# Forgetting-attention values in three float32r passes, gathered by block of keys

## The chip, the cores and the metric

The kernel runs on one core of a Trainium2 chip. The metric is the device time of one execution in microseconds; a figure for a kernel is the median of its runs. TensorE (PE in the profile) multiplies matrices, its weight loads are listed apart as PEld; VectorE is DVE, ScalarE is ACT, GpSimd is POOL, and SP issues the loads of the weights.

## What is computed

The reference is a first transformer block and then two layers of a second one, on 512 positions of width 1024. The change is in the attention of the second block's two layers: 8 heads of 128, causal, with a gate per position and head whose logarithms are summed along the sequence (`c` below).

```python
c = jnp.cumsum(log_f, axis=1)
def one_block(args):                   # 128 queries, all 512 keys
    s = jnp.einsum('bhqd,bhkd->bhqk', q_i, k) * scale
    s = s + (c_i[..., :, None] - c[:, :, None, :])
    s = jnp.where(k_pos <= q_pos, s, -jnp.inf)
    p = jax.nn.softmax(s, axis=-1)
    return jnp.einsum('bhqk,bhkd->bhqd', p, v)
...
y_attn = forgetting_attention(q, k, v, log_f) @ w_o_attn[l]
```

In the same layer stand a gated linear recurrence (a convolution of width 4, two gates from block-diagonal products, a scan along the sequence), its output gate, two projections back, and two feed-forward blocks.

## The kernel before

All wide products (GEMMs) are done in three float32r passes: each operand is held as a high part `hi` (a cast to float32r) and a low part `lo` (the difference), and `mm3` issues hi·hi, hi·lo and lo·hi. These are the lines L229, L230 and L231, 512 columns wide. The weights are streamed from memory in chunks of 256 KB through a ring of four buffers: SP loads `raw`, ScalarE casts `hi` (L197), VectorE subtracts `lo` (L198).

`mix(l)` is the layer part that the change touches. It computes the recurrence's input, the gates (`rnn`: products L897 and L898 in plain fp32, two instructions each for 512 columns, their tanh and exp on ScalarE, scans L914 on VectorE), the row of summed gates `ct` (transposed by L1014, written to memory as `cdram`), and then, in two halves `hf` of four heads, the projections q, k and v of those heads. Their accumulators `a` (four banks of PSUM) are emptied by VectorE at L1027, into tiles `qk` for q and k and `v` for v; q and k are normalised and transposed (L393, L395). `attn` runs over the four heads. For each it broadcasts the gate row into `cb` by a DMA from GpSimd's queue (L874), makes score tiles `s` of 128 queries and 128, 256, 384 and 512 keys (`attn_scores`: product L830, gate L833, mask L835, softmax), and one tile behind it the values of each tile (`attn_values`): it transposes the 128x128 blocks of probabilities (L851) into a bank `xs`, copies them to `pT` (L853), and multiplies each block with the head's 128 columns of `v` in plain fp32 (L855), accumulating into a bank `xh`. These are 1+2+3+4 = 10 products of 128 columns per head, 16 heads in both layers. `xh` is copied to `x` (L869). Later, before the last projection `w_o_attn`, all eight outputs are split into hi and lo (L223, L224).

The program is not in the order of the text. A scheduler (Tile) orders each engine's instructions by data dependencies, buffers and priority (`hp` is high priority), so attention, gates and GEMMs are interleaved; each engine then works through its own queue in order, waiting on semaphores. Pools of a fixed number of buffers per name (`t=3, qk=5, v=6, cb=2, s=3, pT=2`) bound how far apart things can run.

Of the kernel before, what the change touches and what calls it, by code (L numbers as in the profile page):

```python
# [7 lines left out]
F32 = mybir.dt.float32  # L8
F32R = mybir.dt.float32r
U8 = mybir.dt.uint8  # L10
AF = mybir.ActivationFunctionType
OP = mybir.AluOpType
# [106 lines left out]
class Build:  # L119
# [721 lines left out]
        nc.vector.tensor_scalar(s, s, ri, None, op0=OP.mult)  # L841
        return st

    def attn_values(self, st, v, vc, i, o):

        nc = self.nc
        n = (i + 1) * 128
        pt = self.aux("xs")
        for j in range(i + 1):
            js = slice(j * 128, j * 128 + 128)  # L850
            nc.tensor.transpose(pt[:, js], st[:, js], self.ident)  # L851
        pT = self.t("pT")
        nc.scalar.copy(pT[:, :n], pt[:, :n])  # L853
        for j in range(i + 1):
            nc.tensor.matmul(o[:, i * 128:n], v[j][:, vc:vc + 128], pT[:, j * 128:j * 128 + 128],  # L855
                             start=(i == 0 and j == 0), stop=(i == 3 and j == 3), skip_group_check=True)

    def attn(self, qT, kT, v, hd0, ct, cdram):

        nc = self.nc  # L860
        out, todo = [], []

        def values(st, hd, i):
            if i == 0:
                out.append(self.aux("xh"))
            self.attn_values(st, v, (hd - hd0) * 128, i, out[-1])
            if i == 3:
                y = self.t("x")
                nc.scalar.copy(y, out[-1])  # L869
                out[-1] = y  # L870

        for hd in range(hd0, hd0 + 4):
            cb = self.t("cb")
            nc.gpsimd.dma_start(cb, cdram[hd:hd + 1, :].to_broadcast([128, 512]))  # L874
            for i in range(4):
                todo.append((self.attn_scores(qT[hd - hd0], kT[hd - hd0], i, hd, ct, cb), hd, i))
                if len(todo) > 1:
                    values(*todo.pop(0))
        values(*todo.pop(0))
        return out  # L880

    def rnn(self, xr, bd, l, hb, sp4):
# [66 lines left out]
    def mix(self, l):  # L949
        nc = self.nc  # L950
        h = self.hx
        with ExitStack() as ctx:
            lp = ctx.enter_context(self.tc.tile_pool(name=f"lp{l}", bufs=1))
            self.pool(ctx, f"mb{l}", hm=8, t=3, bq=1, qk=5, v=6, qkT=8, cb=2, s=3, pT=2)
            with self.hp():
                rt, rb = self.stats()
            hb = self.lined(lp, (128, 32), name="hb")
# [13 lines left out]
            ct = self.lined(lp, (128, 32), name="ct")  # L971
            cdram = self.dp.tile([8, 512], F32, name=f"cd{l}")
            with ExitStack() as c2:
# [12 lines left out]
                for m in range(0, 8, 2):  # L986
                    for a in self.pair("w_in_2", l, 8, MIX + m * 128, h):
                        y = scaled(a, "t")
# [9 lines left out]
            for k0 in (0, 4):  # L998
                hi, lo = self.w("w_in_2", l, k0, 4, 3072, 128)
# [14 lines left out]
                nc.tensor.transpose(ps[:, i * 8:i * 8 + 8], fc[:, i * 128:i * 128 + 128], self.ident[0:8, 0:8])  # L1014
            nc.vector.tensor_copy(ct, ps[:, 0:32])
            self.tap(f"fc{l}", fc)
            ya = []
            for hf in range(2):
                for n in range(3):
                    bq = self.t("bq")  # L1020
                    c = n * 1024 + hf * 512
                    nc.gpsimd.dma_start(bq, self.ap["brow"][l:l + 1, c:c + 512].to_broadcast([128, 512]))
                    ts = []
                    for tt, a in enumerate(self.tokens("w_in_2", l, c, h)):
                        v = self.t("v" if n == 2 else "qk")
                        with self.hp():
                            nc.vector.scalar_tensor_tensor(v, a, rt[:, tt:tt + 1], bq, op0=OP.mult, op1=OP.add)  # L1027
                        ts.append(v)
                    if n == 0:
                        qT = self.heads_T(ts, 4, 128, qg)  # L1030
                    elif n == 1:
                        kT = self.heads_T(ts, 4, 128, self.col(("k_norm_2", l)))
# [19 lines left out]
            for n, (o, wn) in enumerate(((3072, "w_o_rnn_2"), (2048, "w_o_attn_2"))):  # L1052
# [4 lines left out]
                for m in range(0, 8, 2):  # L1057
                    ga = self.pair("w_in_2", l, 8, MIX + o + m * 128, h)
                    yo = self.pair(wn, l, 8, m * 128, yh if n else yr)
                    for i in range(2):  # L1060
                        with self.hp():
                            s = scaled(ga[i], "t" if n else "hm")
# [109 lines left out]
```

## Time and profile before

| what | value |
|---|---|
| runs | 3414.32 to 3415.7 us, median 3415.19 us |
| profiled execution | 3415.62 us |
| span of its trace | 3413.8 us |
| PE busy | 3393.3 us (99%) |
| DVE busy | 1880.3 us (55%) |
| ACT busy | 1308.8 us (38%) |

The profiled execution is 1.8 us longer than the span that the trace covers, and 0.4 us over the median. A busy engine is one with an instruction in progress; matmuls are pipelined, so that consecutive ones overlap in the rows, and what one adds to the time is the distance from its start to the next start. The chain that ended last gives PE 97% of the span, DVE 2% and ACT 1%.

### The profile page before, as it was taken

What the parts mean: (1) busy time and instruction counts of PE and PEld (TensorE: products, weight loads), DVE (VectorE), ACT (ScalarE), POOL (GpSimd) and SP (SyncE); (2) the same over time, 40 slices, a digit from 0 to 9 for tenths busy, and PEclk for the clock granted to TensorE, in tenths of its full rate; (3) what the DMA queues carried; (4) which work ended last, traced back from release to release, by engine and by line L of the source; (5) the groups of instructions that cost most, each with busy time, mean ns of one, the idle gap of its engine ahead of it and who ended that gap; (6) DMA issues with size and microseconds to landing.
All of it is one profiled execution on the core that took longest, in us unless ns stands there. A gap on an engine that the chain in (4) does not pass through costs nothing.

```text
span 3413.8 us, 42019 instructions
## 1 busy us (share of the span) xinstructions
PE 3393.3 (99%) x15370; PEld 2769.7 (81%) x15370; DVE 1880.3 (55%) x3168; ACT 1308.8 (38%) x2284; POOL 164.6 (5%) x273
## 2 busy tenths in 40 slices
PE   9999999999999999999999999999999999999999
PEld 6887777888888888788888888888887788888887
DVE  7698654534444444876455444444447865454442
ACT  3335443423333333654333333333336544343331
POOL 0011100000000001121000000000010110000000
PEclk9999999999999999999999999999999999999999
DMA  6223533433333333232333333333333222433332
GB/s 217 72 75 105 155 112 111 130 96 97 98 95 94 97 118 106 89 91 90 112 96 96 97 98 96 96 97 99 102 124 94 87 90 81 122 95 99 96 104 91
DMA packets 179599, 351.30 MB, mean 103 GB/s; under 512 B 20672, under 2 KB 21952, under 8 KB 178368
## 3 DMA queue, kind: packets, MB, share of 16 engines
q1 hardware_dynamic: 172944, 328.53, 31.5%
q0 software_dynamic: 6160, 19.37, 1.9%
q8 instruction: 121, 1.98, 0.2%
q10 hardware_dynamic: 288, 0.72, 0.1%
q14 instruction: 86, 0.70, 0.1%
HBM read 342.21 MB, written 6.32 MB: 102 GB/s over the span
## 4 chain that ended last, share of the span: by engine, by line
PE 97%; DVE 2%; ACT 1%; issue 0%; DMA 0%; POOL 0%; SPq 0%; DVEq 0%; ACTq 0%
PE a L231 30%; PE a L229 30%; PE a L230 30%; PE xh L855 1%; PE xs L830 1%; PE xh L430 1%; PE xh L512 1%; PE xs L490 1%; PE xs L851 1%; PE xm L393 0%; DVE xc L895 0%; PE xh L506 0%; PE xh L469 0%; PE xs L897 0%; PE xs L898 0%
## 5 line engine op out<-in xcount | busy, mean ns | idle before, releaser
L198 DVE TENSOR_TENSOR lo<-raw,hi 128x512 fp32r<-128x512 f32 x1144 | 785.8, 688 | 1255.9 <-ACT hi L197 1240.4
L197 ACT CAST hi<-raw 128x512 fp32r<-128x512 f32 x1144 | 707.1, 619 | 1569.4 <-PE a L230 1271.2
L230 PE MATMUL a<-h,hi 128*128 128x512 f32 x2528 | 990.3, 392 | 0.0
L229 PE MATMUL a<-h,hi 128*128 128x512 f32 x2528 | 984.6, 392 | 2.3 <-ACT h L590 2.3
L231 PE MATMUL a<-h,lo 128*128 128x512 f32 x2528 | 983.3, 393 | 0.0
L229 PEld LDWEIGHTS a<-h,hi 128*128 128x128 f32 x2528 | 475.5, 188 | 106.1 <-issue 6.1
L231 PEld LDWEIGHTS a<-h,lo 128*128 128x128 f32 x2528 | 475.2, 188 | 105.4 <-issue 7.2
L230 PEld LDWEIGHTS a<-h,hi 128*128 128x128 f32 x2528 | 475.2, 188 | 101.5 <-issue 3.6
L229 PE MATMUL a<-act,hi 128*128 128x512 f32 x960 | 373.4, 389 | 0.0
L230 PE MATMUL a<-act,hi 128*128 128x512 f32 x960 | 373.4, 389 | 0.0
L231 PE MATMUL a<-act,lo 128*128 128x512 f32 x960 | 372.8, 389 | 0.0
L230 PE MATMUL a<-Y,hi 128*128 128x512 f32 x544 | 214.5, 394 | 0.0
L229 PE MATMUL a<-Y,hi 128*128 128x512 f32 x544 | 213.7, 393 | 0.0
L231 PE MATMUL a<-Y,lo 128*128 128x512 f32 x544 | 212.8, 391 | 0.0
L230 PEld LDWEIGHTS a<-act,hi 128*128 128x128 f32 x960 | 180.2, 188 | 37.4
L229 PEld LDWEIGHTS a<-act,hi 128*128 128x128 f32 x960 | 180.2, 188 | 37.4
L231 PEld LDWEIGHTS a<-act,lo 128*128 128x128 f32 x960 | 180.2, 188 | 37.4
L231 PE MATMUL a<-hi,h 128*128 128x512 f32 x512 | 204.6, 403 | 0.0
L230 PE MATMUL a<-lo,h 128*128 128x512 f32 x512 | 203.7, 398 | 0.0
L229 PE MATMUL a<-hi,h 128*128 128x512 f32 x512 | 199.2, 407 | 1.7 <-DVE qk L1027 1.7
L231 PEld LDWEIGHTS a<-Y,lo 128*128 128x128 f32 x544 | 102.2, 188 | 23.6 <-issue 2.1
L230 PEld LDWEIGHTS a<-Y,hi 128*128 128x128 f32 x544 | 102.1, 188 | 22.9 <-issue 2.0
(290 smaller groups left out, 3056.7 us busy)
## 6 DMA issues: line engine op xcount, KB each, us to landing
raw<-in_w_l SPq DMA_DIRECT2D x852, 256.0 KB, 2.6
raw<-in_w_first SPq DMA_DIRECT2D x284, 256.0 KB, 2.6
mr<-in_mod_b_ SPq DMA_DIRECT2D x32, 512.0 KB, 3.8
mq<-in_mod_a SPq DMA_DIRECT2D x8, 1024.0 KB, 7.5
xs<-x POOLq DMA_DIRECT2D x16, 256.0 KB, 2.3
cb<-cd POOLq DMA_DIRECT2D x16, 256.0 KB, 3.5
x<-xs POOLq DMA_DIRECT2D x16, 256.0 KB, 3.8
bq<-in_brow POOLq DMA_DIRECT2D x12, 256.0 KB, 3.8
```

The source lines that it names most:

```text
L197: nc.scalar.copy(hi, raw)
L198: nc.vector.tensor_tensor(lo, raw, hi.bitcast(F32), op=OP.subtract)
L229: mm(acc, w[0], x[0], start=start, stop=False)
L230: mm(acc, w[0], x[1], start=False, stop=False)
L231: mm(acc, w[1], x[0], start=False, stop=stop)
L430: mm(ps[:, i * 64:i * 64 + 64], k[:, s], q[:, s].rearrange("p (n c h) -> p n c h", c=2, h=h)[:, :, 1], start=True, stop=True)
L490: mm(z[:, o:o + n], q[pr, blk(i)], k[pr, :n], start=True, stop=True)
L512: mm(pt[pr, c], v[j][:, hd * 64:hd * 64 + 64], f[:, o + j * 128:o + j * 128 + 128], start=j == 0, stop=j == i, skip_group_check=True)
L830: nc.tensor.matmul(ps[:, :n], qT[:, ts], kT[:, :n], start=True, stop=True)
L851: nc.tensor.transpose(pt[:, js], st[:, js], self.ident)
L855: nc.tensor.matmul(o[:, i * 128:n], v[j][:, vc:vc + 128], pT[:, j * 128:j * 128 + 128], start=(i == 0 and j == 0), stop=(i == 3 and j == 3 ...
```

## The change

Values are no longer made per block of queries. All score tiles of a head are kept (`s` has five buffers), and `attn_values` runs once per head, over the four blocks j of 128 keys: it transposes that block of all score tiles which see it (4, 3, 2, 1 blocks), casts the result to `hi`, subtracts `lo`, and accumulates in three float32r passes over 512, 384, 256 and 128 columns. `v` is split into `hi` and `lo` after it is emptied into a tile `qk`, and lives in eight float32r tiles of a pool that is opened only after the gate row. The values of a head are issued in the middle of the next head's scores. The names `t`, `cb`, `v` and `s` get other numbers of buffers. Lines behind the change in the file have numbers lower by 4 (L1014 becomes L1010, L897 becomes L893, L913 and L914 become L909 and L910, L1027 becomes L1024, L198 stays).

```diff
@@ -841,42 +841,38 @@
         nc.vector.tensor_scalar(s, s, ri, None, op0=OP.mult)
         return st
 
-    def attn_values(self, st, v, vc, i, o):
-
-        nc = self.nc
-        n = (i + 1) * 128
-        pt = self.aux("xs")
-        for j in range(i + 1):
+    def attn_values(self, sts, v, vc):
+
+        nc = self.nc
+        o = self.aux("xh")
+        for j in range(4):
             js = slice(j * 128, j * 128 + 128)
-            nc.tensor.transpose(pt[:, js], st[:, js], self.ident)
-        pT = self.t("pT")
-        nc.scalar.copy(pT[:, :n], pt[:, :n])
-        for j in range(i + 1):
-            nc.tensor.matmul(o[:, i * 128:n], v[j][:, vc:vc + 128], pT[:, j * 128:j * 128 + 128],
-                             start=(i == 0 and j == 0), stop=(i == 3 and j == 3), skip_group_check=True)
+            n = 512 - j * 128
+            pt = self.aux("xs")
+            for i in range(j, 4):
+                nc.tensor.transpose(pt[:, (i - j) * 128:(i - j) * 128 + 128], sts[i][:, js], self.ident)
+            hi, lo = self.t("pT", F32R), self.t("pT", F32R)
+            nc.scalar.copy(hi[:, :n], pt[:, :n])
+            nc.vector.tensor_tensor(lo[:, :n], pt[:, :n], hi[:, :n].bitcast(F32), op=OP.subtract)
+            self.mm3(o[:, j * 128:], [a[:, vc:vc + 128] for a in v[j]], (hi[:, :n], lo[:, :n]), j == 0, j == 3)
+        y = self.t("x")
+        nc.scalar.copy(y, o)
+        return y
 
     def attn(self, qT, kT, v, hd0, ct, cdram):
 
         nc = self.nc
         out, todo = [], []
-
-        def values(st, hd, i):
-            if i == 0:
-                out.append(self.aux("xh"))
-            self.attn_values(st, v, (hd - hd0) * 128, i, out[-1])
-            if i == 3:
-                y = self.t("x")
-                nc.scalar.copy(y, out[-1])
-                out[-1] = y
-
         for hd in range(hd0, hd0 + 4):
             cb = self.t("cb")
             nc.gpsimd.dma_start(cb, cdram[hd:hd + 1, :].to_broadcast([128, 512]))
+            sts = []
             for i in range(4):
-                todo.append((self.attn_scores(qT[hd - hd0], kT[hd - hd0], i, hd, ct, cb), hd, i))
-                if len(todo) > 1:
-                    values(*todo.pop(0))
-        values(*todo.pop(0))
+                sts.append(self.attn_scores(qT[hd - hd0], kT[hd - hd0], i, hd, ct, cb))
+                if i == 1 and todo:
+                    out.append(self.attn_values(*todo.pop(0)))
+            todo.append((sts, v, (hd - hd0) * 128))
+        out.append(self.attn_values(*todo.pop(0)))
         return out
 
     def rnn(self, xr, bd, l, hb, sp4):
@@ -951,7 +947,7 @@
         h = self.hx
         with ExitStack() as ctx:
             lp = ctx.enter_context(self.tc.tile_pool(name=f"lp{l}", bufs=1))
-            self.pool(ctx, f"mb{l}", hm=8, t=3, bq=1, qk=5, v=6, qkT=8, cb=2, s=3, pT=2)
+            self.pool(ctx, f"mb{l}", hm=8, t=2, bq=1, qk=5, qkT=8, cb=1, s=5, pT=2)
             with self.hp():
                 rt, rb = self.stats()
             hb = self.lined(lp, (128, 32), name="hb")
@@ -1014,6 +1010,7 @@
                 nc.tensor.transpose(ps[:, i * 8:i * 8 + 8], fc[:, i * 128:i * 128 + 128], self.ident[0:8, 0:8])
             nc.vector.tensor_copy(ct, ps[:, 0:32])
             self.tap(f"fc{l}", fc)
+            self.pool(ctx, f"at{l}", v=8)
             ya = []
             for hf in range(2):
                 for n in range(3):
@@ -1022,10 +1019,10 @@
                     nc.gpsimd.dma_start(bq, self.ap["brow"][l:l + 1, c:c + 512].to_broadcast([128, 512]))
                     ts = []
                     for tt, a in enumerate(self.tokens("w_in_2", l, c, h)):
-                        v = self.t("v" if n == 2 else "qk")
+                        v = self.t("qk")
                         with self.hp():
                             nc.vector.scalar_tensor_tensor(v, a, rt[:, tt:tt + 1], bq, op0=OP.mult, op1=OP.add)
-                        ts.append(v)
+                            ts.append(self.split(v, "v") if n == 2 else v)
                     if n == 0:
                         qT = self.heads_T(ts, 4, 128, qg)
                     elif n == 1:
```

The scheduler moves instructions as a result. The first place is on TensorE, in the first layer, where the gate row is transposed (L1014 before, L1010 after; `xm` is the bank, `s2392` the row of gates). Around it stands the GEMM of q (accumulators `a2395` to `a2398`). Before:

```order
L229 MATMUL a2398_11235<-hi2406_11274,h2154_10144 128x512
L230 MATMUL a2398_11235<-lo2407_11275,h2154_10144 128x512
L1014 MATMUL xm2393_11224<-cst_74,s2392_11214 128x8 [waits DVE_49]
L1014 MATMUL xm2393_11224<-cst_74,s2392_11214 128x8 x3
L231 MATMUL a2398_11235<-hi2406_11274,h2155_10145 128x512
L230 MATMUL a2395_11232<-lo2410_11293,h2158_10155 128x512
L231 MATMUL a2395_11232<-hi2409_11292,h2159_10156 128x512
L229 MATMUL a2396_11233<-hi2409_11292,h2158_10155 128x512
```

After the change, with the waits on other engines in brackets:

```order
L230 MATMUL a2397_11237<-lo2410_11296,h2158_10155 128x512
L231 MATMUL a2397_11237<-hi2409_11295,h2159_10156 128x512
L1010 MATMUL xm2393_11224<-cst_74,s2392_11214 128x8 [waits DVE_49]
L1010 MATMUL xm2393_11224<-cst_74,s2392_11214 128x8 x3
L893 MATMUL xs2342_11035<-xc2341_11030,bd2251_10638 128x512 [waits DVE_49,Activation_49]
L894 MATMUL xs2343_11036<-xc2341_11030,bd2253_10646 128x512 [waits Activation_49]
L229 MATMUL a2398_11238<-hi2400_11241,h2111_9922 128x512 [waits DVE_49]
L230 MATMUL a2398_11238<-lo2401_11242,h2111_9922 128x512
```

The gates' products of the third convolution tile (L893 and L894, input `xc2341`) now stand directly behind the transposes; before, they stand 27 rows further down, behind GEMM passes.

The second place is on VectorE, where the four accumulators of v are emptied (`a2491` to `a2494`) and where the recurrence's last four scans stand (`hm2360` and others; L913/L909 multiplies, L914/L910 scans). Before:

```order
L1027 SCALAR_TENSOR_TENSOR v2519_11794<-a2491_11646,m2248_10617,bq2490_11644 128x512
L198 TENSOR_TENSOR lo2657_12218<-raw2655_12215,hi2656_12217 128x512
L1027 SCALAR_TENSOR_TENSOR v2520_11796<-a2492_11647,m2248_10617,bq2490_11644 128x512
L1027 SCALAR_TENSOR_TENSOR v2521_11798<-a2493_11648,m2248_10617,bq2490_11644 128x512
L1027 SCALAR_TENSOR_TENSOR v2522_11800<-a2494_11649,m2248_10617,bq2490_11644 128x512
L906 SCALAR_TENSOR_TENSOR abc2379_11151<-abc2379_11151,xc2376_11142 128x512
L905 SCALAR_TENSOR_TENSOR abc2380_11152<-xc2382_11158,abc2380_11152 128x512
L913 TENSOR_TENSOR abc2358_11091<-abc2358_11091,abc2359_11092 128x512
L913 TENSOR_TENSOR abc2365_11111<-abc2365_11111,abc2366_11112 128x512
L833 SCALAR_TENSOR_TENSOR s2525_11806<-xs2524_11804,ct_10633,cb2523_11802 128x128
L914 SCALAR_TENSOR_TENSOR hm2360_11093<-hm2360_11093,abc2358_11091 128x512
```

After:

```order
L909 TENSOR_TENSOR abc2358_11091<-abc2358_11091,abc2359_11092 128x512
L909 TENSOR_TENSOR abc2365_11111<-abc2365_11111,abc2366_11112 128x512
L909 TENSOR_TENSOR abc2372_11131<-abc2372_11131,abc2373_11132 128x512
L198 TENSOR_TENSOR lo2675_12241<-raw2673_12238,hi2674_12240 128x512
L910 SCALAR_TENSOR_TENSOR hm2360_11093<-hm2360_11093,abc2358_11091 128x512
L909 TENSOR_TENSOR abc2379_11151<-abc2379_11151,abc2380_11152 128x512
L910 SCALAR_TENSOR_TENSOR hm2367_11113<-hm2367_11113,abc2365_11111 128x512
L198 TENSOR_TENSOR lo2678_12259<-raw2676_12256,hi2677_12258 128x512
L910 SCALAR_TENSOR_TENSOR hm2374_11133<-hm2374_11133,abc2372_11131 128x512
L910 SCALAR_TENSOR_TENSOR hm2381_11153<-hm2381_11153,abc2379_11151 128x512
L1024 SCALAR_TENSOR_TENSOR qk2519_11797<-a2491_11649,m2248_10617,bq2490_11647 128x512
```

The four emptyings stood ahead of the scans; now the first of them stands behind all four multiplications, all four scans and two `lo` of weights, and goes into a tile `qk`.

The third place is on TensorE, at the last head of the layer (accumulator `xh2924` before, `xh2978` after) with the GEMM that the scheduler put next to it. Before, the last products:

```order
L230 MATMUL a3062_13915<-Y2664_12262,hi3065_13919 128x512
L855 MATMUL xh2924_13262<-pT2942_13317,v2816_12945 128x128 [waits Activation_49]
L855 MATMUL xh2924_13262<-pT2942_13317,v2817_12947 128x128
L855 MATMUL xh2924_13262<-pT2942_13317,v2818_12949 128x128
L855 MATMUL xh2924_13262<-pT2942_13317,v2819_12951 128x128
L231 MATMUL a3062_13915<-Y2663_12261,lo3066_13920 128x512 [waits DVE_49]
L229 MATMUL a3062_13915<-Y2667_12275,hi3065_13919 128x512
L230 MATMUL a3062_13915<-Y2668_12276,hi3065_13919 128x512
```

After the change, the end of the last head, and what follows (`Y3170`, `Y3171`, `Y3156` are hi and lo parts of attention outputs, `hi3198` weights of `w_o_attn`):

```order
L230 MATMUL xh2978_13395<-pT2987_13423,v2847_13018 128x256 [waits DVE_49]
L231 MATMUL xh2978_13395<-pT2986_13422,v2848_13019 128x256
L229 MATMUL xh2978_13395<-pT2989_13431,v2850_13024 128x128 [waits Activation_49]
L230 MATMUL xh2978_13395<-pT2990_13432,v2850_13024 128x128 [waits DVE_49]
L231 MATMUL xh2978_13395<-pT2989_13431,v2851_13025 128x128
L229 MATMUL a3186_14374<-Y3170_14296,hi3198_14432 128x512 [waits Activation_49]
L229 MATMUL a3187_14375<-Y3170_14296,hi3198_14432 128x512
L230 MATMUL a3186_14374<-Y3171_14297,hi3198_14432 128x512 [waits DVE_49]
L231 MATMUL a3186_14374<-Y3170_14296,lo3199_14433 128x512
L230 MATMUL a3187_14375<-Y3171_14297,hi3198_14432 128x512
L231 MATMUL a3187_14375<-Y3170_14296,lo3199_14433 128x512
L229 MATMUL a3216_14532<-Y3156_14268,hi3219_14536 128x512 [waits DVE_49]
```

Before, other GEMM passes of the output gates follow and the first use of `w_o_attn` is about 190 rows further down. Now the passes of `w_o_attn` follow immediately, and they wait for the casts of the attention's output.

## Rows read from the trace of the kernel before

**Rows 1.** First lines of the page: span, and the engines over all of it.

```profile
span 3413.8 us, 42019 instructions
...
PE 3393.3 (99%) x15370; PEld 2769.7 (81%) x15370; DVE 1880.3 (55%) x3168; ACT 1308.8 (38%) x2284; POOL 164.6 (5%) x273
```

**Rows 2.** Busy us by stretches: PE, PEld, DVE, ACT, POOL; then clock, DMA share, GB/s.

```profile
1000.00:1100.00 100.00, 100.00 (x443) 82.84 (x442) 47.45 (x73) 32.15 (x54) 0.00 (x0) 1.00 0.33 100
...
1400.00:1500.00 100.00, 98.76 (x458) 78.31 (x458) 84.01 (x154) 60.58 (x110) 12.52 (x16) 1.00 0.29 90
...
1450.00:1480.00 30.00, 30.00 (x146) 24.71 (x145) 29.52 (x61) 16.90 (x36) 4.98 (x6) 1.00 0.36 105
```

**Rows 3.** Who TensorE waited for: us in all, times, longest.

```profile
PE a L229 <- DVE qk L1027: 1.7, 2, 0.9
...
PE xm L393 <- ACT qkT L395: 0.8, 2, 0.4
```

**Rows 4.** TensorE in order of time, first head of attention: start us, us, instruction.

```profile
1456.79 0.27 PE L851 MATMUL xs<-cst,s 128*128 128x128 f32 x1
1456.90 0.81 PE L830 MATMUL xs<-qkT,qkT 128*128 128x384 f32 x2
...
1461.88 0.38 PE L855 MATMUL xh<-pT,v 128*128 128x128 f32 x2
1462.10 0.38 PE L851 MATMUL xs<-cst,s 128*128 128x128 f32 x2
```

**Rows 5.** Line L855, the products of the values.

```profile
L855 PE MATMUL xh<-pT,v x320: 270/275/275, 1461.9 to 2886.4; 128*128 128x128 f32 x160
```

**Rows 6.** TensorE in order of time, at the transposes of the gate row.

```profile
1368.38 0.41 PE L1014 MATMUL xm<-cst,s 8*128 8x8 f32 x4
1368.72 0.50 PE L231 MATMUL a<-hi,h 128*128 128x512 f32 x1
```

**Rows 7.** VectorE in order of time, same place.

```profile
1368.89 0.75 DVE L895 SCALAR_TENSOR_TENSOR xc<-xr,cv,xc 128x512 f32<-128x512 f32 x1
1369.55 1.29 DVE L198 TENSOR_TENSOR lo<-raw,hi 128x512 fp32r<-128x512 f32 x2
1370.75 0.75 DVE L895 SCALAR_TENSOR_TENSOR xc<-xr,cv,xc 128x512 f32<-128x512 f32 x1
```

**Rows 8.** TensorE in order of time, last gates of the first layer.

```profile
1437.98 1.02 PE L897 MATMUL xs<-xc,bd 128*128 128x512 f32 x2
1438.84 1.02 PE L898 MATMUL xs<-xc,bd 128*128 128x512 f32 x2
```

**Rows 9.** VectorE in order of time, around the same place.

```profile
1437.04 0.75 DVE L1027 SCALAR_TENSOR_TENSOR v<-a,m,bq 128x512 f32<-128x512 f32 x1 [2.08 <-PE a L231]
...
1444.35 1.29 DVE L913 TENSOR_TENSOR abc<-abc,abc 128x512 f32<-128x512 f32 x2 [1.11 <-ACT abc L911]
...
1445.83 1.22 DVE L914 TENSOR_TENSOR_SCAN hm<-hm,abc 128x512 f32<-128x512 f32 x1
1446.96 0.71 DVE L913 TENSOR_TENSOR abc<-abc,abc 128x512 f32<-128x512 f32 x1
1447.59 1.21 DVE L914 TENSOR_TENSOR_SCAN hm<-hm,abc 128x512 f32<-128x512 f32 x1
```

**Rows 10.** Groups by line and form: busy us, mean ns of one, idle before.

```profile
L224 DVE TENSOR_TENSOR Y<-x,Y 128x512 fp32r<-128x512 f32 x8 | 5.5, 688 | 2.7 <-PE a L230 2.6
...
L223 ACT CAST Y<-x 128x512 fp32r<-128x512 f32 x8 | 5.0, 620 | 2.9 <-PE a L230 2.9
...
L869 ACT COPY x<-xh 128x512 f32<-128x512 f32 x8 | 4.7, 581 | 7.0 <-PE xh L855 6.9
...
L853 ACT COPY pT<-xs 128x128 f32<-128x128 f32 x8 | 2.2, 269 | 1.5 <-PE xs L851 1.5
```

**Rows 11.** The broadcast of a gate row: its issue on POOL, and L874 to landing.

```profile
1468.58 0.57 POOL L874 DMA_DIRECT2D cb<-cd  x1 [0.19 <-issue]
...
DMA to landing us min/median/max: 3.3/3.5/4.4
```

## The prediction

> **What bounds the kernel now.** I read the head of the page first, then the windows, the waits of TensorE, and the timelines of the places that the change touches. The page shows TensorE busy for 3393.3 of 3413.8 us [rows 1]: it leaves 20 us in all, so the time is TensorE's work plus the few places where it stands still. The windows say the same by stretches: in a stretch of GEMMs alone, 443 float32r passes of 512 columns fill 100 us at a granted clock of 1.00, the upper level of 2.4 GHz, so one pass costs 0.226 us; in the stretch with gates and attention TensorE still has 98.76 of 100 us, while VectorE is at 84.01, and between 1450 and 1480 us VectorE has 29.52 of 30 [rows 2]. The wait list shows how little of the mix is lost: 1.7 us in two waits at the emptying of accumulators and 0.8 us in two at transposes, over both layers [rows 3]. So the prediction has two parts: what TensorE's work becomes, and which new waits arise in an order that had almost none.
>
> **The products removed.** In the first head, a product of values starts at 1461.88 and the next instruction at 1462.10: 0.22 us for one product of 128 columns, in two instructions [rows 4]. There are 160 of them, listed as 320 instructions [rows 5], so 35.2 us are removed. The transposes stay: 10 blocks per head either way.
>
> **The products added.** Each head now has 12 passes: three each of 512, 384, 256 and 128 columns. No float32r pass narrower than 512 columns is in the trace, so I bound it. By columns from 0.226 us [rows 2] the passes cost 0.226, 0.170 and 0.113 us, and the narrowest would cost 0.057, but every instruction of 128 columns in the trace, a transpose or half of an fp32 product, takes 0.11 us from start to start (1456.79 to 1456.90, and half of 0.22) [rows 4]. With 0.11 a head costs 3 x (0.226 + 0.170 + 0.113 + 0.110) = 1.86 us, all 16 heads 29.7, a gain of 5.5 us. If the narrowest pass costs what an fp32 product of its size does, 0.22, a head costs 2.19 us, all 35.0, a gain of 0.2 us. Between these ends neither is nearer, so I take the middle, a gain of 2.9 us.
>
> **The work beside it.** ScalarE's four copies per head become casts of four widths, the same total of columns. VectorE gains four subtractions per head (about 1.8 us, from 0.688 us for 512 columns by width [rows 10]) and four of v per half (2.8 us), so 10 us per half; ScalarE gains four casts of 0.620 us per half [rows 10]. Their cover is TensorE's GEMM work between. It is thin only where VectorE is already full [rows 2], which is the third rival. `cb` with one buffer means that a gate row is fetched only when the last score tile of the head before has been read: 0.57 us of issue and 3.5 us to landing [rows 11], 4.1 us in which GpSimd's queue holds the issue and VectorE's queue soon stands at the next gate addition, with `lo` parts of weights behind it. The cover is the weights already split; I count it at nothing, and with the third rival if the cover is gone.
>
> **The waits added.** Both layers have the same order, so each is counted twice.
>
> (a) The gates behind the transposed gate row. TensorE comes to L1014 at 1368.38 and goes on at 1368.72 [rows 6]. The next instruction will be the gates' product of `xc2341`, whose last convolution tap starts at 1370.75 now, with two `lo` (1.20 us) between it and the tap of 1368.89 [rows 7]. In the new order the two taps follow each other: the last starts at about 1369.55 and is ready at 1370.3. TensorE arrives at 1368.7, so it waits 1.6 us. Bounds: 1.0 if VectorE gets there a tap earlier, 2.4 if the `lo` of the following chunk, now behind the gates on VectorE, is late too.
>
> (b) The first emptying of v. Counted from 1439.70, where TensorE is through with the layer's last gates (L898 starts at 1438.84 and takes 0.86, as L897 did from 1437.98 [rows 8]), the first multiplication of the recurrence's end starts at 1444.35 [rows 9], 4.65 us later. In the new order VectorE then has four multiplications (0.61 each), four scans (1.13 each, 1445.83 to 1446.96), two `lo` (0.60 each, half of 1.20 [rows 7]) and the emptying, 0.75 [rows 9], before the accumulator is free: 4.65 + 2.4 + 4.5 + 1.2 + 0.75 = 13.5 us. Before, the emptying stood ahead of that and was begun at 1437.04. TensorE arrives at the first GEMM pass that needs this bank after 48 passes (10.85 us), eight transposes (0.88) and two score products (0.22 and 0.43, by columns from 0.86), 12.4 us. It waits 1.1 us; bounds 0 (VectorE 1.1 us quicker somewhere in that row) and 3 (the other three emptyings go through one spare `qk` tile each).
>
> (c) The end of the layer. The last head ended far from the first use of `w_o_attn`; now its passes stand directly ahead of it, and nothing is left to put between. The last block's cast to `hi` stands behind a weight's cast on ScalarE (about 0.5 us of wait), `lo` on VectorE follows (0.6), then the copy of the output, 0.581 us, and its cast, 0.620 [rows 10], with 0.3 of handing over: 1.5 us in which TensorE has nothing. Then 0.25 us for the output's `lo`, 0.688 less the two passes in front of it, and 0.5 until an accumulator is free: 3.3 us in all, of which the 0.5, 0.3 and 0.5 are estimates (about one ScalarE or VectorE instruction of these rows, or half of one, each). Bounds: 1.5 if only copy and cast remain, 4.5 if a weight's cast comes between each of them. A block's copy of 128 columns takes 0.269 us [rows 10], so the chain itself is not longer.
>
> (d) `t` with two buffers and the evictions of q and k, where waits of 0.9 and 0.4 us stand already [rows 3]: 0.6 us per layer, bounds 0 and 2.
>
> The sum is 1.6 + 1.1 + 3.3 + 0.6 = 6.6 us per layer, 13.2 in both, bounds 5 and 24. The profiled execution took 3415.6 us, 1.8 more than its span and 0.4 more than the median of the runs: 3415.6 - 2.9 + 13.2 = 3425.9, against the median 3425.5. With all bounds it would be 3414.7 to 3439.
>
> **A rule weighed.** The rows give 0.226 us for a pass of 512 columns in a running stream. The Trainium skill, TensorE: Matmul & The Clock Gate, section Back-to-back issue gap, gives for the isolated gap at full clock N/2.4 + 2.5 ns, by which 512, 384, 256 and 128 columns take an estimated 216, 162, 109 and 56 ns; a head would take 1.63 us and the gain would be 9.1 us. The trace has 226 where that has 216, and for 128 columns 110 where that has 56, so here the measurement decides; the sum stays at 2.9.
>
> **The rivals.** First: the waits are mostly covered and the narrow passes are cheap, because the semaphores named in the new order are met early by engines that run ahead. For it speaks that waits in the present order are 1.3 us per layer in all [rows 3]; against it, that the inputs of (a) and (c) are late by the trace's own times. The time is about 3415.2 - 5.5 + 5 = 3414.7, no change that shows: 0.2%, 6.8 us, is about what a measurement of this kernel can tell from none.
>
> Second, on the other side, faster: a narrow pass costs by its columns alone. Then a head costs 3 x (0.226 + 0.170 + 0.113 + 0.057) = 1.70 us, all 27.1, a gain of 8.1 us, 3407.1 without waits. It decides only if all new waits stay under 1.3 us (8.1 less 6.8), and (c) alone is more by its lower bound. Against it stands the 0.11 us of each 128-column instruction [rows 4].
>
> Third: VectorE becomes the bound in the first half of each layer. The 10 us more, with waits of up to 4.1 us for each gate row in front of `lo` parts, fall where it has 29.52 of 30 us [rows 2]. Uncovered, they put 20 us on the two layers, and with (a) and (c), 9.8, it is 3415.2 - 2.9 + 29.8 = 3442. Against it: over the whole first half TensorE's work between the same marks grows too, since GEMM passes are put there.
>
> Fourth: all float32r passes under 512 columns cost what fp32 does (0.86 us for 512 columns [rows 8]): 0.226 + 0.65 + 0.43 + 0.22, three times, 4.58 us per head, 73.3 in all, 38 more than before, with the waits 3466. Nothing in the rows speaks for it, but no row excludes it.
>
> **How the numbers follow.** The forecast has 0.56, the first rival 0.25, the second 0.08, the third 0.08, the fourth 0.03. The forecast's own range is 3417 to 3438. From 3411, which takes in the first rival, to 3439, the upper bound of the waits, about 0.8 is held; outside are most of the second, the third and the fourth. Faster is the second rival, 0.08; within 0.2% are the first and a twentieth from the forecast's lower end, 0.30; slower is the rest, 0.62.
>
> **What the changed profile would show.** The passes that read `pT`: starts 0.226, 0.17, 0.11 and 0.11 to 0.22 us apart, and 192 of them in all. A wait of TensorE at L893 of about 1.6 us in each layer, at L229 for the emptying L1024 of about 1, and at the last head's `pT`, at the first `Y` and its `lo`. VectorE under 100% between 1450 and 1500 us, or else waits of TensorE at `lo` of weights there. The prediction is wrong if those waits are under half their size, if the narrow passes lie outside 0.06 to 0.22 us, or if waits of more than a microsecond come up at places not named here.

## The result and the profile after

The changed kernel takes 3432.79 us (median of 4 runs, 3432.59 to 3433.16) where the kernel before takes 3415.3 in the same comparison: a ratio of 1.0052, interval 1.004 to 1.0065. It is slower by 17.5 us; forecast were 10.3. The time lies in the range, and the forecast case (new waits, a small gain of the products) is the one that came, but the sum lacked a term of 13 us, and fell only 7 us short because most of its other terms were too dear.

The head of the page of the changed kernel, to be held against [rows 1]:

```profile
span 3431.4 us, 41847 instructions
...
PE 3398.7 (99%) x15242; PEld 2761.9 (80%) x15242; DVE 1916.1 (56%) x3248; ACT 1317.1 (38%) x2300; POOL 158.2 (5%) x273
```

TensorE is busy 5.4 us longer with 128 instructions fewer, and stands still 12.2 us longer (3431.4 less 3398.7, against 20.5 before). Both need an explanation. The list of who TensorE waited for (us in all, times, longest; rows before: [rows 3]):

```profile
PE a L229 <- DVE qk L1024: 4.1, 6, 1.1
...
PE xs L893 <- DVE ct L1011: 3.6, 2, 1.8
...
PE a L229 <- ACT Y L223: 2.6, 2, 1.3
...
PE xh L230 <- DVE pT L856: 0.9, 2, 0.4
PE xh L229 <- ACT pT L855: 0.7, 2, 0.3
PE xs L893 <- DVE xc L891: 0.7, 2, 0.3
```

All of these are new or larger, and each comes equally often in both layers (the first three times in each, the others once). The releaser of the second row is named as `ct`, the last thing VectorE did; what L893 reads is `xc`, whose last tap ends at 1369.04 us, 0.1 us ahead of the copy to `ct`. The first of the two places, on TensorE in order of time (start, us, instruction, wait before it; before: [rows 6]), and the same stretch by windows of 2 us (last three columns: granted clock, DMA share, GB/s):

```profile
1367.00 0.41 PE L1010 MATMUL xm<-cst,s 8*128 8x8 f32 x4
1369.19 2.05 PE L893 MATMUL xs<-xc,bd 128*128 128x512 f32 x2 [1.78 <-DVE ct L1011]
1371.03 1.74 PE L894 MATMUL xs<-xc,bd 128*128 128x512 f32 x2
1371.95 1.04 PE L229 MATMUL a<-hi,h 128*128 128x512 f32 x1
```

```profile
1366.00:1368.00 2.00, 1.41 (x9) 0.88 (x7) 2.00 (x4) 0.83 (x2) 0.56 (x1) 1.00 0.05 8
1368.00:1370.00 2.00, 0.81 (x1) 0.50 (x2) 1.21 (x4) 0.72 (x1) 0.10 (x1) 0.76 0.40 129
1370.00:1372.00 2.00, 2.00 (x5) 0.79 (x3) 1.04 (x2) 0.69 (x2) 0.00 (x0) 0.50 0.01 2
1372.00:1374.00 2.00, 2.00 (x9) 1.37 (x8) 0.47 (x1) 2.00 (x3) 0.00 (x0) 0.89 0.00 0
```

The wait is 1.78 us, 1.6 was forecast. What follows it was not forecast: the granted clock falls to 0.50, the lower level of 1.2 GHz, and L893 takes 1.84 us from start to start where L897 took 0.86 [rows 8]. In these windows the clock is missing 0.24, 0.50 and 0.11 of 2 us each, 1.7 us.

The end of the layer, in the same two views:

```profile
1721.46 0.33 PE L229 MATMUL xh<-pT,v 128*128 128x128 f32 x1 [0.34 <-ACT pT L855]
1722.22 0.33 PE L230 MATMUL xh<-pT,v 128*128 128x128 f32 x1 [0.43 <-DVE pT L856]
...
1723.98 1.21 PE L229 MATMUL a<-Y,hi 128*128 128x512 f32 x2 [1.32 <-ACT Y L223]
1724.99 0.63 PE L230 MATMUL a<-Y,hi 128*128 128x512 f32 x1
1725.41 0.63 PE L231 MATMUL a<-Y,lo 128*128 128x512 f32 x1
```

```profile
1722.00:1724.00 2.00, 0.46 (x3) 0.31 (x3) 0.20 (x2) 1.20 (x2) 0.00 (x0) 1.00 0.44 123
1724.00:1726.00 2.00, 2.00 (x5) 1.57 (x6) 0.66 (x1) 0.00 (x0) 0.55 (x1) 0.51 0.02 8
1726.00:1728.00 2.00, 2.00 (x7) 1.16 (x6) 1.88 (x3) 0.62 (x1) 0.00 (x0) 0.64 0.42 131
```

Here TensorE waits 2.1 us in three pieces (3.3 was forecast), and then runs at 0.51 and 0.64: passes of 512 columns stand 0.42 to 0.43 us apart instead of 0.226 [rows 2], 1.7 us more. That is the distance which the Trainium skill, TensorE: Matmul & The Clock Gate, section Back-to-back issue gap, gives for the cold clock (N/1.2, an estimated 427 ns); the trace agrees.

The emptying of v, forecast at 1.1 us, came as forecast and left the clock alone. It cost a restart besides: the first pass behind it takes 0.50 us to its end, where in the stream each pass ends 0.227 us behind the one before, so 0.27 us more (the ends of matmul rows are modelled).

```profile
1446.81 0.50 PE L229 MATMUL a<-h,hi 128*128 128x512 f32 x1 [1.11 <-DVE qk L1024]
1447.14 0.40 PE L230 MATMUL a<-h,hi 128*128 128x512 f32 x1
```

The passes of the values, on TensorE in order of time, one pair of each width from the first head:

```profile
1472.00 0.39 PE L230 MATMUL xh<-pT,v 128*128 128x512 f32 x1
1472.23 0.39 PE L231 MATMUL xh<-pT,v 128*128 128x512 f32 x1
...
1477.88 0.34 PE L230 MATMUL xh<-pT,v 128*128 128x384 f32 x1
1478.05 0.34 PE L231 MATMUL xh<-pT,v 128*128 128x384 f32 x1
...
1483.95 0.28 PE L230 MATMUL xh<-pT,v 128*128 128x256 f32 x1
1484.06 0.28 PE L231 MATMUL xh<-pT,v 128*128 128x256 f32 x1
...
1489.52 0.22 PE L230 MATMUL xh<-pT,v 128*128 128x128 f32 x1
1489.58 0.27 PE L231 MATMUL xh<-pT,v 128*128 128x128 f32 x1
```

From start to start they take 0.23, 0.17, 0.11 and 0.06 us: ahead of another pass the price follows the columns down to 128. The third pass of 128 columns, ahead of an fp32 instruction, takes 0.11, and from end to end, with the restarts of two of them behind waits, the 128-column passes take 0.103 us on average.

**Where the 17.5 us are.** The table divides the first layer's mix, from its statistics (L272, 1314.15 us before, 1312.77 after) to the next ones (1824.97 and 1832.86). "Wait" is the time in which no TensorE instruction is in progress; the other columns add, for all TensorE rows of the kind, the distance from the end of the instruction before to its own end, without waits; the 1.2 us of the statistics are in none. For the kernel after, the second layer's length agrees within 0.4 us and its columns within 1.3 (GEMM passes 448.1, gates 15.0); the rest of the span differs by 1.3 us the other way.

| kernel | length | wait | GEMM passes | gates | values | other |
|---|---|---|---|---|---|---|
| before | 510.8 | 1.2 | 443.2 | 13.7 | 17.8 | 33.6 |
| after | 520.1 | 7.0 | 446.8 | 15.9 | 15.0 | 34.3 |
| difference | 9.3 | 5.7 | 3.6 | 2.1 | -2.8 | 0.7 |

So in the first layer the values gain 2.8 us, the waits take 5.7, and 6.3 are work that is unchanged and has become slower (the unrounded columns; 6.7 in the second). Instruction by instruction, against the median of its kind, 1.9 us of the 6.3 lie behind the wait at L893, 2.0 behind the waits at the layer's end, and 1.3 are restarts: the first instruction behind a short wait takes 0.2 to 0.27 us more than its kind (1446.81 above), and there are more of them than before. The last 1.1 is spread over the layer.

### The profile page after: what moved, and what is told of

Same layout as the page of the kernel before. It is cut to its first block, busy times and chain, and to the rows that moved or that the text cites. A ratio compares the mean times of both kernels' runs of the same rounds, so it can differ in the third digit from the quotient of the medians.

```text
span 3431.4 us, 41847 instructions
## 1 busy us (share of the span) xinstructions
PE 3398.7 (99%) x15242; PEld 2761.9 (80%) x15242; DVE 1916.1 (56%) x3248; ACT 1317.1 (38%) x2300; POOL 158.2 (5%) x273
## 4 chain that ended last, share of the span: by engine, by line
PE 94%; DVE 3%; issue 1%; ACT 1%; POOL 0%; DMA 0%; ACTq 0%; DVEq 0%; POOLq 0%
PE a L229 29%; PE a L231 29%; PE a L230 29%; PE xs L830 1%; PE xh L430 1%; PE xh L512 1%; PE xs L490 1%; PE xs L853 1%; DVE xc L891 0%; POOL m L384 0%; PE xh L231 0%; PE xh L230 0%; PE xh L506 0%; PE xm L393 0%; PE xs L893 0%
## 5 line engine op out<-in xcount | busy, mean ns | idle before, releaser
L198 DVE TENSOR_TENSOR lo<-raw,hi 128x512 fp32r<-128x512 f32 x1144 | 785.6, 688 | 1223.6 <-ACT hi L197 1208.6
```

What stands on the lines that cost most here:

```text
L198: nc.vector.tensor_tensor(lo, raw, hi.bitcast(F32), op=OP.subtract)
```

## The experiments

**One number of the pools, in the kernel before.**

```diff
-            self.pool(ctx, f"mb{l}", hm=8, t=3, bq=1, qk=5, v=6, qkT=8, cb=2, s=3, pT=2)
+            self.pool(ctx, f"mb{l}", hm=8, t=2, bq=1, qk=5, v=6, qkT=8, cb=2, s=3, pT=2)
```

> The kernel before with one number changed: the pool of t has two buffers, not three. Theory A (the order and the clock): two buffers alone put the gates' products directly behind the transposed gate row and the emptying of v behind the scans, as in the changed kernel. Per layer the wait at the gates is 1.8 us, its restart 0.3 and a stretch at the lower clock behind it 1.6; the emptying 1.1 and 0.3; small ones 0.6: 5.7 us per layer, so about 3426.5 us, and a granted clock near 0.91 between 1360 and 1380 us. Theory B (waits alone cost, the clock falls for another reason, such as the mix of fp32 and float32r): 3.5 us per layer, about 3422 us, clock 1.00 there. Theory C (the new order comes from the gathered values, not from t): no change, 3415 us.

Measured: 3427.28 us, ratio 1.0035 (1.0023 to 1.0048). With values in plain fp32 and nothing of the new attention, the wait of 1.78 us is there in both layers. TensorE in order of time, and windows at the wait of the first layer, at that layer's end, and at the wait of the second layer:

```profile
1368.26 0.41 PE L1014 MATMUL xm<-cst,s 8*128 8x8 f32 x4
1370.44 1.10 PE L897 MATMUL xs<-xc,bd 128*128 128x512 f32 x2 [1.78 <-DVE ct L1015]
```

```profile
1360.00:1380.00 20.00, 18.22 (x69) 13.13 (x69) 14.70 (x24) 14.67 (x22) 1.90 (x5) 0.91 0.27 80
1720.00:1740.00 20.00, 20.00 (x89) 16.55 (x89) 8.75 (x14) 6.31 (x10) 0.00 (x0) 1.00 0.36 102
...
2600.00:2630.00 30.00, 28.11 (x117) 21.08 (x116) 21.91 (x37) 22.79 (x34) 1.90 (x5) 1.00 0.26 79
```

Behind the first wait the clock falls, behind the second it does not, though the order and the wait are the same: the first layer takes 517.3 us, the second 515.7. The 1.6 us between them are what the lower clock costs, by itself. So two buffers of `t` make the new order of the gates and of the emptying of v, and 12 to 13 us; theory B's 3422 and theory C's 3415 are out, and theory A is right in the sum, with a clock drop that does not come every time. The five runs lie 4.5 us apart (3424.01 to 3428.52) where the nine of the kernel before lie within 1.8; a price that is not paid every time would do that, but only the profiled run shows its clock by stretches.

**The same number back in the changed kernel**, and the constant table made smaller so that it fits:

```diff
-        cst = self.lined(cp, (128, 384), name="cst")
-        nc.scalar.dma_start(cst, self.ap["cst"])
+        cst = self.lined(cp, (128, 128), name="cst")
+        nc.scalar.dma_start(cst, self.ap["cst"][:, 0:128])
...
-            self.pool(ctx, f"mb{l}", hm=8, t=2, bq=1, qk=5, qkT=8, cb=1, s=5, pT=2)
+            self.pool(ctx, f"mb{l}", hm=8, t=3, bq=1, qk=5, qkT=8, cb=1, s=5, pT=2)
```

> The changed kernel with three buffers of t again (room is made by loading only the 128 columns of the constant table that are used). Theory A: the wait at the gates, its clock drop and the wait at the emptying of v go, the end of the layer stays: 11 us less than the changed kernel, about 3422 us; clock 1.00 between 1360 and 1380 us and still 0.91 at the end of the layer. Theory B: only the waits come back, about 7 us, 3426 us. Theory C: no change, 3433 us.

Measured: 3427.51 us, ratio 1.0036 (1.0024 to 1.0049): 5.3 us came back, not 11. The clock did what theory A said, at both places (1.00 at the gates, 0.91 at the layer's end), but two new waits of 1.4 and 0.5 us stand near 1448 and 1451 us. Three of v's four emptyings stand behind three of the scans (1451.69 us, the first at 1436.61), and the weight's `lo` that TensorE needs first stands behind two. Two rows of VectorE there, then waits of TensorE, and windows:

```profile
1447.15 1.21 DVE L910 TENSOR_TENSOR_SCAN hm<-hm,abc 128x512 f32<-128x512 f32 x1
1448.28 0.66 DVE L198 TENSOR_TENSOR lo<-raw,hi 128x512 fp32r<-128x512 f32 x1
```

```profile
PE a L231 <- DVE lo L198: 2.8, 2, 1.4
PE a L229 <- ACT Y L223: 2.6, 2, 1.3
...
PE xs L830 <- DVE s L833: 1.0, 2, 0.5
```

```profile
1360.00:1380.00 20.00, 20.00 (x84) 14.93 (x83) 13.37 (x23) 15.02 (x22) 1.25 (x3) 1.00 0.31 102
1720.00:1740.00 20.00, 18.44 (x75) 14.44 (x74) 10.53 (x17) 5.71 (x10) 0.55 (x1) 0.91 0.31 92
```

**Transposes of every second block of keys in the idle bank**, with `t` at two (third) and at three (fourth):

```diff
-            pt = self.aux("xs")
+            pt = self.aux("xm" if j % 2 else "xs")
```

> The changed kernel (with the same smaller constant table, t still two) where the transposes of every second block of keys go to the bank xm, which is idle during attention, so that scores and transposes no longer share two banks. The last head then ends some 220 rows ahead of the first use of w_o_attn. Theory A: the end of the layer loses its waits (2.1 us), restarts (0.8) and the lower clock (1.6), 4.4 us per layer, about 3424 us; clock 1.00 there, still 0.91 at the gates. Theory B: waits alone, 2.1 per layer, 3428.5 us. Rival D (attention is slow because VectorE is full, not because two banks are shared): the last head is as late in time as before, about 3433 us.

> Both: three buffers of t, and every second block's transposes in bank xm. Theory A: what is left is the gain of the products of values, 5.6 us by the trace, and small waits: 3410 to 3412 us, under the kernel before. Theory B: 3432.8 less 7 less 4.2, 3421.5 us. Rival D: VectorE's added subtractions, 10 us per half, cost time of their own: 3417 us or more.

Measured: 3442.61 us (1.0081, 1.0068 to 1.0093) and 3444.43 us (1.0085, 1.0071 to 1.0099). The numbers missed, but for rival D's open "3417 us or more" in the fourth, which holds as a bound only: the ninth experiment below, with as many columns to subtract, is 32 us faster, so the added subtractions are not the cause. The wait at the end of the layer went in both, as said; but the transposes of q and k of the second half use `xm` too, and in the new order they and the last values of the first half stand in one heap at 1533 to 1546 us, with no GEMM pass between; three of their four groups wait there for ScalarE to empty that bank. One of the three, and waits and a window of the third experiment:

```profile
1543.16 1.11 PE L393 MATMUL xm<-cst,qk 128*128 128x128 f32 x4 [0.78 <-ACT qkT L395]
```

```profile
PE xm L393 <- ACT qkT L395: 4.7, 8, 0.8
```

```profile
1540.00:1560.00 20.00, 17.78 (x72) 13.87 (x71) 9.03 (x15) 8.56 (x14) 3.47 (x2) 0.76 0.20 52
```

The clock is missing 4.8 us in this window alone. In the third experiment the wait of 1.78 us at the gates is still there, and the clock stays at 1.00 behind it in both layers. Both theories had counted what the removed waits cost and not what the moved work would meet.

**Two blocks of keys in one bank**, on the second experiment's kernel (its core):

```diff
-        for j in range(4):
-            pt = self.aux("xs")
+        for js in ((0,), (1, 3), (2,)):
+            pt, at, n = self.aux("xs"), {}, 0
```

> The second experiment's kernel (t with three buffers), in which the transposed blocks of keys 1 and 3 (384 and 128 columns) share one bank xs, so a head takes three turns of a bank, three casts and three subtractions for its values instead of four. The last head then ends some 75 rows ahead of the first use of w_o_attn. Theory A: the wait at the end of the layer (1.6 us), its restarts (0.5) and the lower clock behind it (1.6) go, 3.6 us per layer: 3420.3 us, clock 1.00 at 1720 to 1740 us; the wait of 1.4 us at a weight's lo part by 1448 us stays. Theory B (waits only): 3424.3 us. Rival E (attention only moves and waits elsewhere, as in the third and fourth experiments): 3427 us or more.

Measured: 3417.96 us, ratio 1.0009 (1.0 to 1.0017). 9.6 us came back, more than the 7.2 expected: the end of the layer has neither wait nor lower clock, and the values take 14.8 us per layer. The wait at `lo` stays as said, with the same row in the list as in the second experiment (2.8, 2, 1.4). The window at the layer's end:

```profile
1720.00:1740.00 20.00, 20.00 (x90) 16.56 (x89) 8.54 (x13) 5.67 (x10) 0.00 (x0) 1.00 0.34 102
```

**v emptied ahead of the scans**, first into tiles `pT`:

```diff
-            self.pool(ctx, f"mb{l}", hm=8, t=3, bq=1, qk=5, qkT=8, cb=1, s=5, pT=2)
+            self.pool(ctx, f"mb{l}", hm=8, t=3, bq=1, qk=5, v=8, qkT=8, cb=1, pT=2)
...
-            fz, fe, fc = [self.t("s")[0:8] for _ in range(3)]
+            fz, fe, fc = [self.t("v")[0:8] for _ in range(3)]
...
-            self.pool(ctx, f"at{l}", v=8)
+            self.pool(ctx, f"at{l}", s=5)
...
-                        v = self.t("qk")
+                        v = self.t("pT" if n == 2 else "qk")
```

> The fifth kernel, in which v can also be emptied as early as in the kernel before: its eight tiles are in the pool of the layer, it is emptied into a pT tile, and the five score tiles are in the pool that opens behind the gate row instead. The four emptyings stand ahead of the scans again. Theory A: the waits at lo (1.4), at the score tile (0.5) and their restarts go too, and what is left is the gain of the products, 2.8 us per layer, less small waits: 3410 to 3412 us, faster than the kernel before. Rival D (VectorE's added subtractions cost time of their own): 3415 to 3418 us.

Measured: 3427.9 us, ratio 1.0037 (1.0023 to 1.0051). The waits near 1448 us went, and a heap of the last head's values and the second half's transposes arose at 1551 to 1560 us:

```profile
1553.19 0.44 PE L853 MATMUL xs<-cst,s 128*128 128x128 f32 x2 [0.94 <-DVE s L841]
1554.49 0.55 PE L853 MATMUL xs<-cst,s 128*128 128x128 f32 x3 [0.86 <-DVE s L841]
```

```profile
1556.00:1560.00 4.00, 3.96 (x12) 2.77 (x12) 0.91 (x2) 0.76 (x2) 0.00 (x0) 0.50 0.00 0
1560.00:1564.00 4.00, 4.00 (x12) 2.94 (x12) 3.36 (x9) 2.30 (x6) 0.88 (x2) 0.50 0.00 0
```

**The changed kernel with plain fp32 products.**

```diff
-            self.mm3(o[:, j * 128:], [a[:, vc:vc + 128] for a in v[j]], (hi[:, :n], lo[:, :n]), j == 0, j == 3)
+            nc.tensor.matmul(o[:, j * 128:], v[j][0][:, vc:vc + 128].bitcast(F32), hi[:, :n].bitcast(F32),
+                             start=j == 0, stop=j == 3)
```

> The changed kernel (t still two, constant table of 128 columns) with one plain fp32 product of 512, 384, 256 and 128 columns per block of keys in the place of three float32r passes. It multiplies the high parts alone, and leaves the low parts out of the products; the casts and subtractions stay. By the trace its products take 17.3 us per layer (0.86, 0.65, 0.43 and 0.22 for a head) where the passes took 15.0. In its order the last head ends some 190 rows ahead of w_o_attn. Theory A: 3432.8 plus 4.6 for the products, less 7.2 for waits, restarts and clock at the end of the layer: 3430 us, and the clock still falls at 1360 to 1380 us. Theory F (the narrow passes cost as much as fp32 products, and the trace's spacing misleads): 3425.5 us.

Measured: 3427.17 us, ratio 1.0036 (1.0024 to 1.0049), between the two theories' numbers. By the same division as in the table its values take 17.3 us per layer, its GEMM passes 444.6, its waits 4.85: the products cost the 2.3 us more per layer that theory A said, so the narrow passes are cheaper than fp32 and theory F is out as to them; all else gave back 5.1 us per layer (2.8 of the time and 2.3 for the products) in place of 3.6. The clock is 0.91 at 1360 to 1380 us, as said. The kernel is faster than the changed one by 5.6 us with dearer products: between these two the order weighs more than the products. It also drops the passes that wait for `lo`, so it is not the order alone that differs.

**Two buffers of `cb`.**

```diff
-            self.pool(ctx, f"mb{l}", hm=8, t=2, bq=1, qk=5, qkT=8, cb=1, s=5, pT=2)
+            self.pool(ctx, f"mb{l}", hm=8, t=2, bq=1, qk=5, qkT=8, cb=2, s=5, pT=2)
```

> The changed kernel with two buffers of cb again, and nothing else (constant table of 128 columns). The prediction counted the single buffer at nothing. Theory A: within 2 us of the changed kernel, 3433 us. Rival G (VectorE's queue stands at the gate row and makes weights late): 3425 to 3430 us.

Measured: 3433.57 us, ratio 1.0053 (1.0041 to 1.0066), as the changed kernel; all its waits are there. The single gate row costs nothing.

**v emptied ahead into `t`, into `qk`, and with another pairing of blocks.** The ninth and tenth differ from the sixth in one word each, the eleventh from the ninth in the groups:

```diff
-                        v = self.t("pT" if n == 2 else "qk")
+                        v = self.t("t" if n == 2 else "qk")
```

> As the sixth experiment, but v is emptied into a tile of t, not of pT. In the sixth, emptyings of the second half held the two pT tiles that the last values of the first half needed, and TensorE stood still four times by 1551 to 1555 us, with the clock falling behind it. Theory A: v stands ahead of the scans, neither end bunches, no clock drop in the mix; per layer 3.0 us of products gained, 0.5 to 1.5 lost in small waits and restarts: 3411 to 3413 us, faster than the kernel before. Rival D (VectorE's added work costs time of its own): 3415 to 3418 us. Rival E (a wait turns up elsewhere again): above 3418 us, with a new wait of over 1 us in the list.

> As the ninth, with v emptied into tiles qk, as in the changed kernel: three emptyings stand ahead of the scans, the fourth behind. Theory A: 3412 to 3415 us; a small wait at the fourth emptying. Rival E: above 3418 us.

> As the ninth, with the transposed blocks of keys 2 and 3 in one bank (256 and 128 columns) instead of 1 and 3. Theory A: the same time as the ninth within 2 us.

Measured: 3412.47 us (0.9992, 0.9983 to 1.0001), 3413.31 us (0.9994, 0.9985 to 1.0003), 3412.84 us (0.9993, 0.9984 to 1.0001), each against 3415.28 of the kernel before. The numbers came as theory A said; the small wait that the tenth was to have at the fourth emptying is not in its list, which has 0.2 us at a `lo` instead. The ninth is 20 us under the changed kernel and its median is 2.8 us under the kernel before, which the interval does not separate from no change. Its waits and windows:

```profile
PE a L229 <- DVE qk L1027: 1.7, 2, 0.9
...
PE xh L230 <- DVE pT L857: 0.8, 2, 0.4
```

```profile
1360.00:1380.00 20.00, 20.00 (x84) 14.93 (x83) 13.38 (x23) 15.22 (x23) 1.36 (x4) 1.00 0.36 107
...
1720.00:1740.00 20.00, 20.00 (x90) 16.54 (x89) 8.30 (x13) 4.91 (x8) 0.00 (x0) 1.00 0.34 92
```

The layer's division for it: length 509.7, wait 1.6, GEMM 444.0, gates 13.7, values 15.1, other 33.9. The gain of the values is all there, 2.7 us, and 1.5 of it goes in waits, restarts and changes between the kinds of product.

## Why the prediction was right, and where its size was off

**The products.** The middle price, a gain of 2.9 us over both layers, was mis-sized: it is 5.6 (17.8 less 15.0 per layer), the cheap end of the bounds, 5.5. What failed is the step to the middle, which let the narrowest pass cost up to 0.22 us: it takes 0.103 on average. That the gain met the cheap end so closely is partly luck, for 0.11 us is no floor: the pass takes 0.06 from start to start when a float32r pass follows it and 0.11 when another kind does, and two restarts at the last head, 0.5 us per layer, and slightly dearer wide passes (0.231 for 0.226) make up the rest. The four distances of 0.23, 0.17, 0.11 and 0.06 lie near the 216, 162, 109 and 56 ns by the rule of the Trainium skill for the isolated gap that the prediction set aside (TensorE: Matmul & The Clock Gate, Back-to-back issue gap); for the narrow passes the trace agrees with it. The second rival's price, by columns alone, holds for a pass ahead of another, but its gain of 8.1 us and its condition, no new waits, did not come.

**The waits.** Per layer 6.6 us were forecast, and 5.7 came: (a) 1.78 for 1.6, (b) 1.11 for 1.1, (c) 2.1 for 3.3, (d) 0.7 for 0.6 (2.0 in small waits less 1.24 before, of which 0.3 stands at a gates' product that (d) did not name). The second experiment takes (a) away, the sixth, ninth and tenth take (b) and the fifth takes (c) by orders in which the late input is early, as the steps said. Of (c), the last block's `hi` took 0.34 us for 0.5, its `lo` 0.43 for 0.6, and the output's copy and cast 1.32 for 1.5; the 0.25 for the output's `lo` and the 0.5 for an accumulator did not come.

**What the sum lacked.** A term for what stands behind a wait: the lower clock, about 1.6 us each at (a) and (c), and 0.27 us for each restart; with the spread rest 6.3 us in the first layer and 6.7 in the second, 13.0 in both. Put in, with the 1.3 us that the rest of the span takes less, the sum reads 3415.6 - 5.6 + 11.4 + 13.0 - 1.3 = 3433.1, against 3433.2 of the profiled execution; it must agree, since its terms are measured there. Waits and products alone would have made 3421.4. The prediction came nearer than that by luck: its products were 2.7 us and its waits 1.8 us too dear, and stood in for part of the missing term. The kernel before had no clock drop in these layers [rows 2], nor at the two places:

```profile
1360.00:1380.00 20.00, 20.00 (x84) 14.93 (x83) 13.37 (x23) 15.41 (x23) 1.86 (x5) 1.00 0.39 120
1720.00:1740.00 20.00, 20.00 (x90) 16.55 (x89) 8.30 (x14) 5.22 (x9) 0.00 (x0) 1.00 0.34 95
```

**The third rival** (VectorE becomes the bound) did not come as such: with three of the four added subtractions per head, and as many columns, the ninth experiment is no slower than before, and the single `cb` costs nothing. In the second experiment VectorE's queue did make a `lo` late, through the scans ahead of it. **The first rival**'s mechanism, waits that are covered, was no part of the changed kernel; the ninth experiment is what it looks like. **The fourth** is out by the starts of the passes.

**The cause of the order.** The prediction read the new order rightly and did not ask what made it. The first experiment shows that two buffers of `t` alone make (a) and (b); (c) comes with the gathered values: the last head's products end at 1722.38 us in the changed kernel and at 1654.38 before. The third and fifth point to the turns that values and scores take at the two `xs` banks, for with fewer turns there the last head ends at 1680.79 and 1698.13 and (c) is gone; but the fifth has fewer casts and subtractions too, and in the seventh (c) goes as well when the passes no longer wait for `lo` (1691.09). Which of these sets the pace of attention stays open.

**Open.** Which waits bring the clock down is not settled. Behind the same wait of 1.78 us it fell in seven of the ten places where a profile has it (both layers of the changed kernel, of the seventh and of the eighth experiment, the first layer of the first) and stayed at 1.00 in three (the second layer of the first, both of the third). In the second experiment 1.4 and 0.5 us near 1448 us left it at 1.00, and 1.3 us at the layer's end did not. So 1.6 us per wait is a price that is paid or not, and a forecast should carry it as a range.

## What to carry to other kernels

Where one engine is full, the price of a new wait is the wait, its restart and what the clock does behind it: here the second and third together cost nearly as much as the first (5.2 us against 5.7 in the first layer). Changes to the number of buffers made for room can move work that has nothing to do with the edit; compare the order of an old part that nobody meant to touch, as here the gates, before costing the new part. And work taken off one shared bank meets other work at the next: look at who uses that bank half a layer later.

## What the runs showed of the hardware that was not expected

A float32r pass of 128 columns takes 0.06 us from start to start ahead of another one (1489.52 to 1489.58), half of what an fp32 instruction of that size takes (0.11, [rows 4]); ahead of an fp32 instruction it takes 0.11 too. The granted clock fell to 0.50 at a single wait of 1.78 us in seven of ten places, not in the other three, and was back after 3 to 4 us; in these layers it was below 1.00 only in stretches that began during a wait or within 1.5 us behind one. The first instruction behind a wait of 0.3 to 1.1 us takes 0.2 to 0.27 us more than its kind (0.50 us to its end at 1446.81, against 0.227).
